# One VectorE for the norm steps, constants in TensorE's waits, and bias rows that are copied per head

## The chip, the cores and the metric

The kernel runs on one core of a Trainium2 chip. The metric is the device time of one execution in microseconds (us); the time before is a median of three runs. TensorE is called PE here, VectorE DVE, ScalarE ACT, GpSimd POOL, and SyncE, whose queue loads the weights, SP.

## The reference, cut to what matters

256 tokens of 1024 values, with 16 meta tokens ahead of them, pass through two layers of a first model and one of a second. A layer of the first model ends each of its halves with a norm that is added to the stream, and the next half begins with another norm of the sum:

```python
def rms_norm(x, g):
    y = xf * lax.rsqrt(jnp.mean(xf * xf, axis=-1, keepdims=True) + EPS)
    return (y * g).astype(x.dtype)

for l in range(DEPTH):                       # 2 layers
    u = rms_norm(h, norm_mix_pre[l])
    proj = u @ w_in[l]                       # retention and attention branches, gates
    ...
    mix = (sigmoid(gate_r) * y_r + sigmoid(gate_a) * y_a) @ w_mix_o[l]
    h = h + rms_norm(mix, norm_mix_post[l])
    u = rms_norm(h, norm_ff_pre[l])
    ff = square(relu(u @ w_ff1[l])) @ w_ff2[l]
    h = h + rms_norm(ff, norm_ff_post[l])
```

The second model projects the 256 tokens to eight stick-breaking and eight dilated heads (the latter with a bias from a table of 32 buckets by distance), multiplies by `w_out`, normalizes, chooses two of 16 experts for each token (`softmax`, best group of four, best two in it), and adds the experts' gated products. All inputs are float32.

## The kernel before, in words

Everything is held with features on the 128 partitions and tokens along the free dimension: `h` has 8 blocks (`KB`) of 128 features by 272 tokens (`L`), or 256 where the meta tokens are no longer needed (`c0`, `s`). The 128x1024 weight blocks (512 KB each) come in order through `Stream` on SP's queue, into four `raw` buffers; `parts` (L72) cuts each in two halves of 512 columns and splits them in a high part `wh` (ACT, L79) and a low part `wl` (L80), three buffers of each. `get` may be told the two engines that make the halves of `wl`: the input projections (`project`, L338, for the blocks 3 to 16), the mixer's `project` (L832) and `w_out` give the second half to POOL, all others have DVE for both.

A dense product takes three passes of a weight block over the tokens, `mm3` (L99): `wh` with the high part of the tokens (L106), `wh` with their low part (L107), `wl` with their high part (L108). 24 of them make an output block of 128 features. Where three output blocks run side by side at the start of a stage (`project`, `ff1`), they take each feature block `kb` in turn, so that PE can begin with the first feature block of a norm.

Four times PE waits for a norm: after the mixing product and after the second feed-forward product of both layers. `sumsq` (L138) sums the squares of the product's blocks, `token_rs` (L153) sums over features with a product of constants (`c_mean`, L159 and L160) and computes 1/sqrt with ACT's logarithm and exponential and one Newton step (`newton`, L166, into `rs_b`). `add_to_h` (L759) then scales the product `f`, adds it to `h` and splits the result into `uh` and `ul` (`xh` and `xl` ahead of the mixer) for the next product. It makes the first block by a way of its own: POOL computes `hg` (L765) and `fy` (L768) beside the Newton step, DVE finishes with L770 and L773. For the other blocks each engine scales (L780) and adds (L781); POOL does the blocks 3 and 6, DVE the rest; ACT makes `uh` (L787) and DVE `ul` (L788). The squares of the new `h` are summed on POOL (L148), for the next norm's factor, which is multiplied in behind the product.

The bias of the dilated heads has one row of 384 values per head (`bias_rows`, L267), formed from the table in the first layer's gates. One DMA on ACT's queue (L279) writes each of the 8 rows 128 times to `scratch` in DRAM, and a later load reads a band with shifted rows from it (`band`, in `mixer_constants`, L221).

The router (L1227 on) forms the choice of experts on DVE out of PE's logits (`po`, L1101), takes counts by products, and gathers each expert's tokens by products (L1274). The weights of the experts, 201 MB, are then loaded in order into buffers that the mixer gave back.

The order on each engine is set by a scheduler that takes the code's order and its dependencies; `add_manual_dep` adds an order without a wait. No table is written out by hand.

Of the kernel before, what the change touches and what calls it, by code (L numbers as in the profile page):

```python
# [19 lines left out]
KB = 8  # L20
META = 16
SEQ = 256
# [23 lines left out]
EXP_LN_SET = 6  # L46
WEIGHTS = ["early"] * 2 + ["early2"] + ["big"] * 8 + ["big2"] * 3 + ["big", "big2"] + ["ring"] * 3 + ["big"] + ["ring2"] * 3
# [39 lines left out]
class Kern:  # L87
    def __init__(self, tc, a, out, dbg=None):
        self.tc, self.nc, self.a, self.out, self.dbg = tc, tc.nc, a, out, dbg or {}
        self.naux = self.ndense = 0  # L90
        self.h_on_pool = None
# [46 lines left out]
    def sumsq(self, acc, src, kb, c0, engine):  # L138
# [9 lines left out]
        x = engine.tensor_tensor(acc[:, c0:], acc[:, c0:], sq[:, c0:], op=ALU.add)  # L148
        if engine is nc.gpsimd and self.h_on_pool is not None:
            self.tc.add_manual_dep(x.ins, self.h_on_pool.ins.name, self.nosync, reason="the sums' own part first")  # L150
        return None

    def token_rs(self, acc, sq, c0):  # L153
# [6 lines left out]
        nc.tensor.matmul(pb[:, :n], self.c_mean, sq[:, c0:], start=False, stop=True)  # L160
# [106 lines left out]
    def bias_rows(self):  # L267
# [9 lines left out]
        nc.vector.tensor_tensor(row[:SB], ps[:SB, :384], lc[:SB], op=ALU.add)  # L277
        self.scratch = self.dram.tile([SB, 128, 384], F32, name="scratch")
        nc.scalar.dma_start(self.scratch, row[:SB].unsqueeze(1).broadcast_to([SB, 128, 384]))  # L279


    def first_layer(self, l):
# [43 lines left out]
        def pre_norm():  # L326
            acc = tp.tile([128, L], F32, name="acc", bufs=1)
            for kb in range(KB):
                sq = self.sumsq(acc, h[:, kb], kb, 0, nc.gpsimd if l else nc.vector)
# [8 lines left out]
        def project(names, s):  # L338
# [5 lines left out]
            both = (nc.vector, nc.gpsimd) if 3 <= done[0] <= 16 else None  # L344
            ws = [st.get(base + C_IN + j, engines=both, after=self.norm_steps if len(c) == 3 == j + 1 else None) for j in c]
            pts = [self.dense_tile() if done[0] < 7 else self.mm_tile() for _ in c]
            for kb in range(KB):
                for (wh, wl), ps in zip(ws, pts):
                    self.mm3(ps[:, :L - s], (hi(wh), hi(wl)), (lambda k: uh[:, k, s:], lambda k: ul[:, k, s:]),
                             [(kb, kb)], kb == 0, kb == KB - 1)  # L350
# [343 lines left out]
        def out_blocks(f, acc, blocks, first_chunk, nk, x, g):  # L694
# [8 lines left out]
            for b, ps in zip(blocks, pts):  # L703
                sq = self.sumsq(acc, ps[:, :n], b, c0, nc.vector)
# [9 lines left out]
        rs1 = self.token_rs(acc, sq, c0)  # L714
# [7 lines left out]
        ux = (lambda k: uh[:, k, c0:], lambda k: ul[:, k, c0:])  # L722

        def ff1(blocks):
            ws = [st.get(base + C_FF1 + b, after=self.norm_steps if b == 2 else None) for b in blocks]
            pts = [self.dense_tile() for _ in blocks]
            for kb in range(8):
                for (wh, wl), ps in zip(ws, pts):
                    self.mm3(ps[:, :n], (hi(wh), hi(wl)), ux, [(kb, kb)], kb == 0, kb == 7)
# [11 lines left out]
        for kb in range(KB):  # L741
            sq = self.sumsq(acc2, h[:, kb, c0:], kb, c0, nc.gpsimd)
# [13 lines left out]
        rs3 = self.token_rs(acc, sq, c0)  # L756
        self.pending = (f, rs3, c0)

    def add_to_h(self, f, rs, c0, uh, ul, g=None, s=0):  # L759

        nc, h = self.nc, self.h
        r, (_, y, t) = rs, rs
        hg = self.tmp("hg", tag="Q", bufs=2)
        g0 = 1.0 if g is None else g[:, :1]
        nc.gpsimd.tensor_scalar(hg, h[:, 0], g0, None, op0=ALU.mult)  # L765

        fy = self.tmp("fy")
        nc.gpsimd.tensor_tensor(fy[:, c0:], f[:, 0, c0:], y[:, c0:], op=ALU.mult)  # L768
        a = self.tmp("t_h")
        nc.vector.scalar_tensor_tensor(a[:, c0:], t[:, c0:], 1.5, fy[:, c0:], op0=ALU.add, op1=ALU.mult)  # L770
        if s < c0:
            nc.scalar.activation(uh[:, 0, :c0 - s], hg[:, s:c0], AF.Copy)
        x = nc.vector.scalar_tensor_tensor(uh[:, 0, c0 - s:], a[:, c0:], g0, hg[:, c0:], op0=ALU.mult, op1=ALU.add)  # L773
        self.norm_steps.append(x)
        rs = self.newton(r, c0)
        for kb in range(KB):
            e = nc.gpsimd if kb in (3, 6) else nc.vector
            if kb:
                a = self.tmp("t_h")
                e.tensor_tensor(a[:, c0:], f[:, kb, c0:], rs[:, c0:], op=ALU.mult)  # L780
            x = e.tensor_tensor(h[:, kb, c0:], h[:, kb, c0:], a[:, c0:], op=ALU.add)  # L781
            if kb == 6:
                self.h_on_pool = x
            x = h[:, kb, s:]
            gk = 1.0 if g is None else g[:, kb:kb + 1]
            if kb:
                nc.scalar.activation(uh[:, kb], x, AF.Copy, scale=gk)  # L787
            nc.vector.scalar_tensor_tensor(ul[:, kb], x, gk, uh[:, kb].bitcast(F32), op0=ALU.mult, op1=ALU.subtract)  # L788
# [35 lines left out]
    def mixer(self):  # L824
# [7 lines left out]
        def project(n):  # L832

            both = (nc.vector, nc.gpsimd)
            ws = [st.get(done[0] + j, engines=both, after=self.norm_steps if n == 3 == j + 1 else None) for j in range(n)]
            done[0] += n
            pts = [self.mm_tile() for _ in ws]
            for kb in range(KB):
                for (wh, wl), ps in zip(ws, pts):
                    self.mm3(ps[:, :SEQ], (hi(wh), hi(wl)), (lambda k: xh[:, k], lambda k: xl[:, k]),  # L840
                             [(kb, kb)], kb == 0, kb == KB - 1)
# [247 lines left out]
        def routed(j):  # L1089

            xt2 = st.raw_pool.tile([128, 1024], F32, name="raw", bufs=st.n_raw)
            for jj in range(2):
# [6 lines left out]
                for i in range(4):  # L1099
                    kb, t = 4 * j + 2 * jj + i // 2, i % 2  # L1100
                    mm(pl[:, NE * t:NE * t + NE], xt[:, 128 * i:128 * i + 128], self.wr[:, kb],  # L1101
                       start=(i == jj == j == 0), stop=(kb == KB - 1), skip_group_check=True)

        for half in range(2):
            for c in range(4):
# [3 lines left out]
                wh, wl = st.parts(w_out[4 * half + c], 256, (nc.vector, nc.gpsimd))  # L1109
                for kb in range(4):  # L1110
                    for t in range(2):
                        ps = po[t][c // 2][:, 256 * (c % 2):256 * (c % 2) + 256]
                        yh, yl = (y[half][:, i, kb, 128 * t:128 * t + 128] for i in range(2))
                        mm(ps, yh, wh[:, kb], start=False, stop=False, skip_group_check=True)
                        mm(ps, yl, wh[:, kb], start=False, stop=False, skip_group_check=True)
                        mm(ps, yh, wl[:, kb], start=False, stop=(half == 1 and kb == 3), skip_group_check=True)
# [64 lines left out]
    def router(self):  # L1181
# [43 lines left out]

        pp = self.bank("pu_")
# [316 lines left out]
    def run(self):  # L1543
        tc, nc = self.tc, self.nc
        pool = lambda name, bufs=1, **kw: tc.tile_pool(name=name, bufs=bufs, reuse_waits="tile", **kw)
        with pool("cp") as self.cp, pool("hp") as self.hp, pool("dram", space=DRAM) as self.dram, \
# [3 lines left out]
            with pool("big", 10) as self.big, ExitStack() as last, ExitStack() as psum:  # L1550
                self.pp = psum.enter_context(pool("pp", space=PSUM))
                with right("raw") as raw, right("part") as part:
# [166 lines left out]
```

## Time and profile before

| | |
|---|---|
| Median of 3 runs | 1568.73 us (1567.92 to 1570.1) |
| Profiled execution: its own time | 1566.69 us |
| Profiled execution: span | 1564.9 us |
| Granted clock of PE, mean | 0.974 |
| PE busy | 1464.6 us, 94% of the span |
| DVE, ACT, POOL busy | 830.8, 731.2, 138.0 us |
| DMA | 363.84 MB, 232 GB/s over the span |

The page says which engine is busy and which stretches lose time. Where a table by stretch is shown, PE's busy time against the length of the stretch is the loss, and the granted clock says whether the products inside run at 2.4 GHz (1.00) or at 1.2 GHz (0.50). A row of a timeline has the start of an instruction, its duration, its engine and its line, and in brackets how long the engine was idle before it and what it waited for. POOL's spans are rough.

### The profile page before, as it was taken

The page shows a single profiled execution, that of the slowest core. Times are in us where ns is not written, and L with a number is a line of the kernel's source. Part 1 is how long each engine was busy: PE and PEld are TensorE (multiplying, and loading weights), DVE is VectorE, ACT ScalarE, POOL GpSimd, SP SyncE. Part 2 cuts the span into 40 slices and gives each one's busy share as a digit, 9 for nine tenths or more (in the row PEclk, how much of TensorE's full clock was granted, in tenths as well). Part 3 has the DMA queues.
Part 4 walks back from the last instruction along what each step waited for, and adds up shares of the span by engine and source line. Part 5 has one row for each costly group of instructions (what it writes and reads, how often), then busy time and mean ns, then how long its engine had stood idle before and what let it go on. Part 6 is the DMA issues. An engine that isn't in the chain of part 4 may idle for free. (4 is left out here: it accounts for less than half of the span.)

```text
span 1564.9 us, 25740 instructions
## 1 busy us (share of the span) xinstructions
PE 1464.6 (94%) x10003; PEld 1150.2 (74%) x10003; DVE 830.8 (53%) x1814; ACT 731.2 (47%) x1646; POOL 138.0 (9%) x132
## 2 busy tenths in 40 slices
PE   7899799899998889999899998999899999999896
PEld 6888699799997788999799997888533334333322
DVE  8877676777445877876787545775301000101002
ACT  7765464566444767674576444875311011101101
POOL 3200000200003320000200003322000000000000
PEclk9999899899998989999899998999999999999999
DMA  6424544365555333445365556547799999999995
GB/s 215 138 97 127 133 138 142 128 195 169 173 174 192 121 122 97 144 152 163 108 202 187 182 186 203 187 162 317 315 419 420 419 420 419 420 419 421 419 419 237
DMA packets 77065, 363.84 MB, mean 232 GB/s; under 512 B 10096, under 2 KB 13192, under 8 KB 52616
## 3 DMA queue, kind: packets, MB, share of 16 engines
q1 hardware_dynamic: 75760, 360.52, 62.5%
q10 hardware_dynamic: 1176, 1.61, 0.9%
q8 instruction: 80, 1.31, 0.3%
q14 instruction: 49, 0.40, 0.1%
HBM read 359.47 MB, written 2.62 MB: 231 GB/s over the span
## 5 line engine op out<-in xcount | busy, mean ns | idle before, releaser
L79 ACT ACTIVATE wh<-raw 128x512 fp32r<-128x512 f32 x576 | 338.6, 625 | 291.6 <-PE mm L107 158.2
L80 DVE TENSOR_TENSOR wl<-raw,wh 128x512 fp32r<-128x512 f32 x519 | 357.2, 710 | 169.4 <-ACT wh L79 160.0
L106 PE MATMUL mm<-uh,wh 128*128 128x272 f32 (+1 forms) x1048 | 312.7, 299 | 21.3 <-DVE uh L773 12.0
L107 PE MATMUL mm<-ul,wh 128*128 128x272 f32 (+1 forms) x1048 | 306.1, 292 | 7.3 <-DVE ul L788 7.3
L108 PE MATMUL mm<-uh,wl 128*128 128x272 f32 (+1 forms) x1048 | 306.4, 292 | 6.1 <-DVE wl L80 4.7
L106 PEld LDWEIGHTS mm<-uh,wh 128*128 128x128 f32 x1048 | 202.9, 194 | 29.5 <-DVE uh L773 13.2
L107 PEld LDWEIGHTS mm<-ul,wh 128*128 128x128 f32 x1048 | 203.0, 194 | 10.0 <-DVE ul L788 8.9
L108 PEld LDWEIGHTS mm<-uh,wl 128*128 128x128 f32 x1048 | 202.7, 193 | 9.2 <-DVE wl L80 7.1
L80 POOL TENSOR_TENSOR wl<-raw,wh 128x512 fp32r<-128x512 f32 x57 | 76.9, 1353 | 453.8 <-ACT wh L79 421.0
L108 PE MATMUL mm<-sh,wl 128*128 128x256 f32 (+1 forms) x352 | 100.3, 285 | 0.0
L107 PE MATMUL mm<-sl,wh 128*128 128x256 f32 (+1 forms) x352 | 100.2, 285 | 0.0
L106 PE MATMUL mm<-sh,wh 128*128 128x256 f32 (+1 forms) x352 | 100.1, 284 | 0.0
L108 PEld LDWEIGHTS mm<-sh,wl 128*128 128x128 f32 x352 | 66.5, 189 | 0.0
L106 PEld LDWEIGHTS mm<-sh,wh 128*128 128x128 f32 x352 | 66.4, 189 | 0.0
L107 PEld LDWEIGHTS mm<-sl,wh 128*128 128x128 f32 x352 | 66.2, 188 | 0.0
L106 PE MATMUL mm<-xh,wh 128*128 128x256 f32 x192 | 55.7, 295 | 6.6 <-DVE xh L773 4.4
L108 PE MATMUL ps<-uh,wl 128*128 128x272 f32 (+1 forms) x200 | 58.4, 292 | 0.3 <-DVE wl L80 0.3
L106 PE MATMUL ps<-uh,wh 128*128 128x272 f32 (+1 forms) x200 | 58.4, 292 | 0.0
L107 PE MATMUL ps<-ul,wh 128*128 128x272 f32 (+1 forms) x200 | 58.2, 291 | 0.0
L107 PE MATMUL mm<-xl,wh 128*128 128x256 f32 x192 | 55.2, 288 | 1.6 <-DVE xl L788 1.6
L108 PE MATMUL mm<-xh,wl 128*128 128x256 f32 x192 | 54.9, 287 | 0.2 <-DVE wl L80 0.2
L108 PE MATMUL ps<-sh,wl 128*128 128x272 f32 (+1 forms) x160 | 45.8, 286 | 0.0
(686 smaller groups left out, 3009.1 us busy)
## 6 DMA issues: line engine op xcount, KB each, us to landing
raw<-in_w_first SPq DMA_DIRECT2D x288, 512.0 KB, 3.5
we_big<-in_w_exp SPq DMA_DIRECT2D x115, 1024.0 KB, 19.9
we_ring<-in_w_exp SPq DMA_DIRECT2D x48, 1024.0 KB, 19.9
we_early<-in_w_exp SPq DMA_DIRECT2D x27, 1024.0 KB, 19.9
wo<-in_w_first SPq DMA_DIRECT2D x4, 512.0 KB, 5.6
we_big<-in_w_exp SPq DMA_DIRECT2D x4, 512.0 KB, 18.1
scratch<-row ACTq DMA_DIRECT2D x1, 1536.0 KB
h<-in_hT SPq DMA_DIRECT2D x4, 272.0 KB, 5.2
```

What stands on the lines that cost most here:

```text
L79: x = nc.scalar.activation(wh[:, c], raw[:, c], AF.Copy)
L80: y = engines[j // 512].tensor_tensor(wl[:, c], raw[:, c], wh[:, c].bitcast(F32), op=ALU.subtract)
L106: mm(ps, wh(kw), xh(kx), start=f, stop=False)
L107: mm(ps, wh(kw), xl(kx), start=False, stop=False)
L108: mm(ps, wl(kw), xh(kx), start=False, stop=l)
```

## The change

Four things change.

*The norm steps.* `add_to_h` works in three steps: `part` (L795 of the new kernel) scales a block of the product, `add` (L800) adds it to `h`, `low` (L803) makes `ul` of the block before. All are on DVE; `hg` moves to ACT. The own way of the first block is left out: its Newton step is done first, then `part` and `uh` (L808). The sums of squares and all halves of `wl` are on DVE too. POOL keeps the retention's distance (L445) and the memsets.

*The order of the products.* `mm3s` replaces `mm3` in the input projections, the first feed-forward product and the mixer's projection. Over the output blocks of a group it issues all `wh` with high parts, then all `wl` with high parts, then all `wh` with low parts. The last chunk of `w_out` goes by token tile instead of by feature block.

*Constants.* `keep_on` issues 13 products of the 128x128 constant `c_mean` with itself, into a PSUM bank that nobody reads. It stands at the start, behind the sum product of the four norms (`token_rs` with `keep`) and in the router behind the logits.

*The bias rows.* The 8 rows go to DRAM once (`bias_row`, ACT's queue). In the first feed-forward product of layer 0, behind the blocks 20 to 27, SP's queue copies one row 128 times to `scratch`, DRAM to DRAM.

```diff
+KEEP = 13
+    def mm3s(self, pts, n, ws, xs, kb, first, last):
+        xh, xl = xs
+        mm = self.nc.tensor.matmul
+        for ps, (wh, wl) in zip(pts, ws):
+            mm(ps[:, :n], wh[:, kb], xh, start=first, stop=False)
+        for ps, (wh, wl) in zip(pts, ws):
+            mm(ps[:, :n], wl[:, kb], xh, start=False, stop=False)
+        for ps, (wh, wl) in zip(pts, ws):
+            mm(ps[:, :n], wh[:, kb], xl, start=False, stop=last)
...
+    def keep_on(self, n, tag, after, psum=None):
+        ps = (psum or self.psum)(tag)
+        for _ in range(n):
+            x = self.nc.tensor.matmul(ps[:, :128], self.c_mean, self.c_mean, start=True, stop=True)
+            if after is not None:
+                self.tc.add_manual_dep(x.ins, after.ins.name, self.nosync, reason="in the wait")
+            after = x
...
-        nc.tensor.matmul(pb[:, :n], self.c_mean, sq[:, c0:], start=False, stop=True)
+        x = nc.tensor.matmul(pb[:, :n], self.c_mean, sq[:, c0:], start=False, stop=True)
+        if keep:
+            self.keep_on(keep, "pz", x)
...
-        nc.scalar.dma_start(self.scratch, row[:SB].unsqueeze(1).broadcast_to([SB, 128, 384]))
+        nc.scalar.dma_start(self.bias_row, row[:SB])
+    def bias_copies(self, hd):
+        self.load(self.scratch[hd:hd + 1], self.bias_row[hd:hd + 1].unsqueeze(1).broadcast_to([1, 128, 384]))
...
-            both = (nc.vector, nc.gpsimd) if 3 <= done[0] <= 16 else None
...
+            if l == 0 and 20 <= b < 28:
+                self.bias_copies(b - 20)
...
-        nc.gpsimd.tensor_scalar(hg, h[:, 0], g0, None, op0=ALU.mult)
-        nc.gpsimd.tensor_tensor(fy[:, c0:], f[:, 0, c0:], y[:, c0:], op=ALU.mult)
-        nc.vector.scalar_tensor_tensor(a[:, c0:], t[:, c0:], 1.5, fy[:, c0:], op0=ALU.add, op1=ALU.mult)
+        nc.scalar.activation(hg, h[:, 0], AF.Copy, scale=gk(0))
+        rs = self.newton(rs, c0)
...
-            e = nc.gpsimd if kb in (3, 6) else nc.vector
...
+        for kb in range(1, KB):
+            part(kb)
+            add(kb)
+            nc.scalar.activation(uh[:, kb], h[:, kb, s:], AF.Copy, scale=gk(kb))
+            low(kb - 1)
+        low(KB - 1)
...
+        self.keep_on(13, "pg_", self.routed, self.bank)
```

**PE, where the mixing product of layer 0 ends and the first feed-forward product begins.** `po` is the bank of the norm's sum, `mm` and `ps` are the banks of the output blocks, `pz` the one of the constants. Before:

```order
L159 MATMUL po<-acc,c_mean 128x272
L160 MATMUL po<-sq,c_mean 128x272
L106 MATMUL mm<-uh,wh 128x272 x2
L106 MATMUL ps<-uh,wh 128x272
L107 MATMUL mm<-ul,wh 128x272
L108 MATMUL mm<-uh,wl 128x272
```

After:

```order
L178 MATMUL po<-acc,c_mean 128x272
L179 MATMUL po<-sq,c_mean 128x272
L167 MATMUL pz<-c_mean 128x128 x13
L116 MATMUL mm<-uh,wh 128x272 x2
L116 MATMUL ps<-uh,wh 128x272
L118 MATMUL mm<-uh,wl 128x272 x2
L120 MATMUL mm<-ul,wh 128x272 x2
```

Behind the sum's product the 13 constants now stand ahead of the first product of the tokens, and the third output block (`ps`) has only its first pass there; its others follow when the first two blocks are done.

**DVE, the same norm.** `rs_*` are the steps of 1/sqrt, `t_h` is the scaled product. Before:

```order
L187 TENSOR_SCALAR rs_h_3516<-po_3510,eps_73 128x272
L189 TENSOR_TENSOR rs_t_3515<-rs_y_3514 128x272
L190 TENSOR_TENSOR rs_t_3515<-rs_t_3515,rs_h_3516 128x272
L770 SCALAR_TENSOR_TENSOR t_h_3528<-rs_t_3515,fy_3526 128x272
L169 SCALAR_TENSOR_TENSOR rs_b_3513<-rs_t_3515,rs_y_3514 128x272
L773 SCALAR_TENSOR_TENSOR uh_3522<-t_h_3528,gvec_66,hg_3524 128x272
L781 TENSOR_TENSOR h_68<-h_68,t_h_3528 128x272
L780 TENSOR_TENSOR t_h_3534<-f_3215,rs_b_3513 128x272
L788 SCALAR_TENSOR_TENSOR ul_3523<-h_68,gvec_66,uh_3522 128x272
L781 TENSOR_TENSOR h_68<-h_68,t_h_3534 128x272
L780 TENSOR_TENSOR t_h_3539<-f_3215,rs_b_3513 128x272
L780 TENSOR_TENSOR t_h_3549<-f_3215,rs_b_3513 128x272
```

After:

```order
L208 TENSOR_SCALAR rs_h_3545<-po_3525,eps_73 128x272
L210 TENSOR_TENSOR rs_t_3544<-rs_y_3543 128x272
L211 TENSOR_TENSOR rs_t_3544<-rs_t_3544,rs_h_3545 128x272
L190 SCALAR_TENSOR_TENSOR rs_b_3542<-rs_t_3544,rs_y_3543 128x272
L795 TENSOR_TENSOR t_h_3556<-f_3230,rs_b_3542 128x272
L808 SCALAR_TENSOR_TENSOR uh_3551<-t_h_3556,gvec_66,hg_3553 128x272
L800 TENSOR_TENSOR h_68<-h_68,t_h_3556 128x272
L795 TENSOR_TENSOR t_h_3560<-f_3230,rs_b_3542 128x272
L803 SCALAR_TENSOR_TENSOR ul_3552<-h_68,gvec_66,uh_3551 128x272
L800 TENSOR_TENSOR h_68<-h_68,t_h_3560 128x272
L795 TENSOR_TENSOR t_h_3565<-f_3230,rs_b_3542 128x272
L795 TENSOR_TENSOR t_h_3570<-f_3230,rs_b_3542 128x272
```

The step that waited for POOL's `fy` (L770) is gone; the first block's scaling stands in its place behind the Newton step, and the blocks follow one another with no place for POOL's.

**SP, the first feed-forward product of layer 0.** `raw` are weight blocks. Before:

```order
L221 DMA lnr_4299<-in_ln_rows 16x256
L64 DMA raw_4303<-in_w_first 128x1024
L64 DMA raw_4342<-in_w_first 128x1024
L64 DMA raw_4381<-in_w_first 128x1024
L64 DMA raw_4420<-in_w_first 128x1024
L64 DMA raw_4459<-in_w_first 128x1024
L64 DMA raw_4498<-in_w_first 128x1024
```

After:

```order
L242 DMA lnr_4326<-in_ln_rows 16x256
L66 DMA raw_4330<-in_w_first 128x1024
L66 DMA raw_4369<-in_w_first 128x1024
L66 DMA raw_4408<-in_w_first 128x1024
L66 DMA raw_4447<-in_w_first 128x1024
L242 DMA scratch_1861<-bias_row_1860 128x1x384
L66 DMA raw_4487<-in_w_first 128x1024
```

A copy of a bias row now stands between two weight blocks, and seven more follow in the same way, one behind each block.

## Rows read from the trace of the kernel before

**Rows 1.** The page, busy us of each engine (share of the span) and instructions:

```profile
PE 1464.6 (94%) x10003; PEld 1150.2 (74%) x10003; DVE 830.8 (53%) x1814; ACT 731.2 (47%) x1646; POOL 138.0 (9%) x132
```

**Rows 2.** Stretches: us; busy PE, PEld, DVE, ACT, POOL; PEclk, DMA share, GB/s.

```profile
154.00:162.00 8.00, 7.86 (x70) 7.25 (x71) 4.83 (x16) 5.11 (x16) 0.00 (x0) 1.00 0.46 59
162.00:180.00 18.00, 8.11 (x66) 7.88 (x64) 6.32 (x20) 4.46 (x13) 0.00 (x0) 0.83 0.66 130
...
340.00:400.00 60.00, 60.00 (x479) 60.00 (x478) 44.74 (x85) 38.17 (x81) 3.10 (x2) 1.00 0.53 171
...
620.00:640.00 20.00, 20.00 (x157) 17.58 (x156) 19.42 (x64) 13.41 (x40) 0.00 (x0) 1.00 0.33 104
```

**Rows 3.** Stretches: each norm, its last L160 product's end to the 97th product.

```profile
286.90:311.26 24.36, 17.70 (x102) 15.98 (x101) 20.89 (x35) 12.09 (x27) 9.65 (x11) 0.79 0.18 59
494.69:520.98 26.29, 17.78 (x102) 15.83 (x101) 20.09 (x31) 13.73 (x31) 13.16 (x14) 0.81 0.13 38
761.93:785.13 23.20, 16.84 (x100) 15.34 (x101) 19.82 (x34) 11.82 (x27) 9.08 (x11) 0.78 0.18 58
956.87:980.25 23.38, 14.93 (x96) 13.89 (x96) 18.09 (x34) 10.15 (x25) 10.10 (x9) 0.78 0.65 216
```

**Rows 4.** Stretches: input projections of layers 0 and 1, and the mixer.

```profile
20.00:80.00 60.00, 51.01 (x367) 48.27 (x366) 53.02 (x95) 44.59 (x99) 20.27 (x16) 0.94 0.41 136
...
520.00:580.00 60.00, 50.32 (x359) 47.52 (x358) 52.70 (x95) 43.64 (x98) 17.98 (x14) 0.91 0.41 132
...
980.00:1100.00 120.00, 116.52 (x916) 105.10 (x917) 80.59 (x207) 86.94 (x215) 34.36 (x28) 1.00 0.63 229
```

**Rows 5.** Stretches: the router, and the expert phase.

```profile
1109.00:1116.00 7.00, 3.41 (x20) 3.35 (x20) 4.20 (x25) 3.05 (x5) 0.00 (x0) 0.51 1.00 421
...
1120.00:1546.00 426.00, 413.01 (x1932) 155.46 (x1930) 41.23 (x88) 51.16 (x96) 0.00 (x0) 1.00 1.01 416
```

**Rows 6.** Timeline of the gates: start, us, engine, line, operation, count [idle <-releaser].

```profile
147.52 1.28 ACTq L279 DMA_DIRECT2D scratch<-row  x1
...
179.49 0.63 ACT L79 ACTIVATE wh<-raw 128x512 fp32r<-128x512 f32 x1 [13.19 <-DMA raw<-in_w_first]
...
180.45 0.90 PE L536 MATMUL pz<-ident,s_a 128*128 128x128 f32 x3 [10.34 <-ACT pt_a L537]
```

**Rows 7.** The page, DMA queue: packets, MB, share of 16 engines.

```profile
q10 hardware_dynamic: 1176, 1.61, 0.9%
```

**Rows 8.** Timeline of the first norm.

```profile
290.64 0.82 PE L106 MATMUL mm<-uh,wh 128*128 128x272 f32 x2 [3.74 <-DVE uh L773]
...
291.29 0.84 POOL L781 TENSOR_TENSOR h<-h,t_h 128x272 f32<-128x272 f32 x1
...
291.43 1.00 DVE L780 TENSOR_TENSOR t_h<-f,rs_b 128x272 f32<-128x272 f32 x1
...
293.40 0.59 PE L107 MATMUL mm<-ul,wh 128*128 128x272 f32 x1 [1.71 <-DVE ul L788]
```

**Rows 9.** Timeline of the second norm, two additions while POOL rests.

```profile
502.87 0.78 DVE L780 TENSOR_TENSOR t_h<-f,rs_b 128x272 f32<-128x272 f32 x2
```

**Rows 10.** Timeline of the router.

```profile
1111.82 0.17 PE L1227 MATMUL pu__13604<-r_mb,utri 128*128 128x16 bf16 x1 [3.34 <-DVE r_mb L1216]
...
1112.87 2.47 PE L1274 MATMUL misc<-sel,x 128*128 128x128 f32 x10 [0.77 <-ACT x L1223]
...
1116.13 1.95 PE L1274 MATMUL pd__13631<-sel,x 128*128 128x128 f32 x16
```

**Rows 11.** Stretches: inside the first norm, right behind its low clock.

```profile
301.00:304.00 3.00, 2.00 (x14) 1.62 (x13) 3.00 (x4) 1.28 (x3) 2.47 (x3) 1.00 0.00 0
```

**Rows 12.** Groups by line: count | busy us, mean ns | idle, releaser.

```profile
L80 POOL TENSOR_TENSOR wl<-raw,wh 128x512 fp32r<-128x512 f32 x11 | 15.0, 1361 | 27.6 <-ACT wh L79 18.2 <-issue 5.9 <-PE mm L108 3.4
L80 POOL TENSOR_TENSOR wl<-raw,wh 128x512 fp32r<-128x512 f32 x12 | 16.8, 1412 | 30.9 <-ACT wh L79 13.1 <-DVE ks_r L368 5.4 <-DVE roped L361 4.7
L80 DVE TENSOR_TENSOR wl<-raw,wh 128x512 fp32r<-128x512 f32 x74 | 49.3, 685 | 11.3 <-ACT wh L79 10.7
```

More of the change, by code (lines that the diff above doesn't have):

```diff
@@ L136, in aux_tile, with sumsq @@
         return self.psum("ps" if self.naux % 2 else "pz")
-    def sumsq(self, acc, src, kb, c0, engine):
+    def sumsq(self, acc, src, kb, c0):
         nc = self.nc
@@ L147, in sumsq, with token_rs @@
             return sq
-        x = engine.tensor_tensor(acc[:, c0:], acc[:, c0:], sq[:, c0:], op=ALU.add)
-        if engine is nc.gpsimd and self.h_on_pool is not None:
-            self.tc.add_manual_dep(x.ins, self.h_on_pool.ins.name, self.nosync, reason="the sums' own part first")
-        return None
-    def token_rs(self, acc, sq, c0):
+        nc.vector.tensor_tensor(acc[:, c0:], acc[:, c0:], sq[:, c0:], op=ALU.add)
+        return None
+    def keep_on(self, n, tag, after, psum=None):
[5 more added lines that the diff above has]
+            after = x
+    def token_rs(self, acc, sq, c0, keep=0):
         nc = self.nc
@@ L343, in project @@
             c = range(done[0] - len(names), done[0])
[L344 to L345 removed]
+            ws = [st.get(base + C_IN + j, after=self.norm_steps if len(c) == 3 == j + 1 else None) for j in c]
             pts = [self.dense_tile() if done[0] < 7 else self.mm_tile() for _ in c]
             for kb in range(KB):
[L348 to L350 removed]
+                self.mm3s(pts, L - s, ws, (uh[:, kb, s:], ul[:, kb, s:]), kb, kb == 0, kb == KB - 1)
             return pts
@@ new lines, in add_to_h, with part, add @@
+        if s < c0:
+            nc.scalar.activation(uh[:, 0, :c0 - s], h[:, 0, s:c0], AF.Copy, scale=gk(0))
+        rs = self.newton(rs, c0)
+        parts = {}
+        def part(kb):
+            a = parts[kb] = self.tmp("t_h")
+            z = nc.vector.tensor_tensor(a[:, c0:], f[:, kb, c0:], rs[:, c0:], op=ALU.mult)
+            if kb:
+                self.tc.add_manual_dep(z.ins, x.ins.name, self.nosync, reason="the first block first")
+        def add(kb):
+            nc.vector.tensor_tensor(h[:, kb, c0:], h[:, kb, c0:], parts[kb][:, c0:], op=ALU.add)
@@ new lines, in low @@
+        def low(kb):
+            nc.vector.scalar_tensor_tensor(ul[:, kb], h[:, kb, s:], gk(kb), uh[:, kb].bitcast(F32), op0=ALU.mult,
+                                           op1=ALU.subtract)
+        part(0)
+        x = nc.vector.scalar_tensor_tensor(uh[:, 0, c0 - s:], parts[0][:, c0:], gk(0), hg[:, c0:], op0=ALU.mult,
+                                           op1=ALU.add)
+        self.norm_steps.append(x)
+        add(0)
+        for kb in range(1, KB):
[3 more added lines that the diff above has]
+            low(kb - 1)
@@ L832, in project @@
         def project(n):
-            both = (nc.vector, nc.gpsimd)
-            ws = [st.get(done[0] + j, engines=both, after=self.norm_steps if n == 3 == j + 1 else None) for j in range(n)]
+            ws = [st.get(done[0] + j, after=self.norm_steps if n == 3 == j + 1 else None) for j in range(n)]
             done[0] += n
@@ L1108, in mixer @@
                         head_scale(k)
[L1109 to L1116, printed above, removed]
+                wh, wl = st.parts(w_out[4 * half + c], 256)
+                ends = half == 1 and c == 3
+                for i in range(8):
+                    kb, t = (i % 4, i // 4) if ends else (i // 2, i % 2)
+                    ps = po[t][c // 2][:, 256 * (c % 2):256 * (c % 2) + 256]
+                    yh, yl = (y[half][:, x, kb, 128 * t:128 * t + 128] for x in range(2))
+                    mm(ps, yh, wh[:, kb], start=False, stop=False, skip_group_check=True)
+                    mm(ps, yl, wh[:, kb], start=False, stop=False, skip_group_check=True)
+                    mm(ps, yh, wl[:, kb], start=False, stop=(half == 1 and kb == 3), skip_group_check=True)
                 if half == 1 and c == 1:
```

45 lines of the change are left out of this document (12 added, 33 removed).

## The prediction

> **What bounds the kernel now.** I read first the busy times of the whole span: PE is busy 1464.6 of 1564.9 us, the other engines about half or less [rows 1]. So a gain can only come from the 100 us in which PE is idle, or from products that run at half clock. Next come stretches: the table by stretch gives for each PE's busy time, the granted clock and the DMA share. A healthy stretch of dense products (340 to 400) reads PE 60.00 of 60 at clock 1.00 [rows 2]. Four kinds of stretch don't: one in the first layer's gates (162 to 180: PE 8.11 of 18, [rows 2]), the four norms that stand between dense stages [rows 3], the input projections of both layers [rows 4], and the router [rows 5]. The change touches all four. After the router the expert phase is bound by DMA (share 1.01 at 416 GB/s over 426 us, [rows 5]): its length doesn't change, but it starts when the mixer's buffers come free, so time won earlier is passed on to the end.
>
> **Part 1, the bias rows.** Before, one DMA on ACT's queue writes 1024 pieces of 1536 bytes from eight partitions at 147.52. From 154 to 162 the DMA engines are 0.46 busy and move only 59 GB/s. ACT then waits 13.19 us for a weight block (until 179.49) and PE 10.34 us (until 180.45) [rows 2, 6]. At the same place in layer 1, where nothing of the kind runs, PE is 20.00 of 20 busy (620 to 640, [rows 2]). The queue's packets took 0.9% of 16 engines' span, 225 us of packet time, or 0.22 us each for the thousand pieces [rows 7]. After: eight rows to DRAM (8 pieces) at this place, so the stall goes. Worth: 10.34 us of waiting, and about 14 products that then run at half clock; a product takes 0.126 us at full clock in the trace's dense stretches (60 us for 479 records [rows 2]) and about twice that at half, so 14 x 0.126 = 1.8. Together 12; lower end 8, if the DMA backlog of the next block is what PE meets instead.
>
> The same 1024 pieces come back as eight copies of 128, ahead of one weight block each, in the first feed-forward product of layer 0, on SP's queue, the one that brings the weights. There PE is at 60.00 of 60 and DMA at 0.53 [rows 2]: of a block's 3.0 us (24 products of 0.126), 1.4 us of DMA time are free. A copy of 128 pieces over 16 engines costs 8 x 0.22 = 1.76 us. The surplus is 0.35 us a block, 2.8 us in all; four raw buffers give 12 us of lead. So I take **0**, and bound it by 0 and 14 us (8 x 1.76, nothing hidden).
>
> A wide spread is what this rests on. Before, the engines' share of 0.46 says that seven or eight of 16 worked, as many as the transfer has source rows [rows 2]. The Trainium skill (DMA: Bandwidth & Descriptors, "Why a DMA increments its semaphore by 16 and not by 1") has the number of engines as the largest divisor up to 16 of the slowest dimension on both sides that isn't of size one. By that rule 8 before, with which the trace agrees, and 16 for the copies, whose leading dimension is one and whose second is 128; no run here shows the copies. The same page ("Queues, rings and completion order") has each engine take a queue's pieces in the order of issue, so a copy on SP's queue holds back the weights behind it in full; that speaks against this part, and by it a copy that isn't hidden costs its whole 1.76 us.
>
> **Part 2, the four norms.** From the end of the last product of the sum of squares to the 97th product behind it, the four take 24.36, 26.29, 23.20 and 23.38 us, of which PE is busy 17.70, 17.78, 16.84 and 14.93 at a mean clock of 0.78 to 0.81 [rows 3]. 96 products at full clock are 12.1 us; the rest is loss. In the first norm PE waits 3.74 us for the first block and 1.71 for its low part [rows 8]. While POOL works on its two blocks, DVE's instructions take 1.00 us (POOL's 0.84 each beside them) [rows 8]; two of the same kind without POOL take 0.78 together [rows 9]. So 0.84 us of POOL costs DVE about 0.57, and PE's feed is DVE.
>
> After: everything is on DVE. Per block a part, an addition and a low part: 0.35 + 0.37 + 0.41 = 1.13 us apart, an estimate from the 0.39 each of [rows 9] and of PE's order. The chain to the first block keeps its length: two instructions of POOL go, one on DVE comes, and the factor (hg) moves to ACT, in a gap that it has before its logarithm. So the first product comes about 3.4 us after the sum instead of 3.74. The other seven blocks at 1.13 are there 11.3 us after the sum, and with the two halves of the third output block's low weights (0.685 each [rows 12]) it is 12.6. In that time PE has the products of two output blocks, 6 x 0.126 = 0.76 us in each 1.13. Some 27 products, nearly all of the third output block, follow at 0.126: 16.0 us. Behind the 72nd product come 24 more, 3.0 us, and 0.8 for the sums of the next norm (an estimate), 3.8 to the 97th: **20.0** us in norms 1 and 2. Norm 3 has 256 columns and gives 19, norm 4 has no sums behind it and gives 18. Gains 4.4, 6.3, 4.2, 5.4: **20 us**. This holds if the clock stays up. 13 products of constants (26 instructions, the 16 of [rows 10] take 1.95 us, so 0.12 each) fill 3.1 us of the 3.4 us wait; they end before the first block is there and push nothing back. At two thirds busy the clock stayed at 1.00 in a stretch right behind [rows 11]. If it falls, the 72 products cost 0.10 us more each where they bound: 27 x 0.10 + the feed 8 x 0.23 = 4.5 us, at most half of it unhidden, so a norm gives about 2.5 less: range 10 to 24.
>
> **Part 3, all low weights on DVE.** In the input projections DVE is 53.02 and 52.70 of 60 busy, and PE 51.01 and 50.32 [rows 4]. POOL makes 11 and 12 low halves there, 15.0 and 16.8 us [rows 12]. They move to DVE at 0.685 us [rows 12]: +7.5 and +8.2. What goes is POOL's share of the slowing, 0.57/0.84 x 15.0 = 10.2 and x 16.8 = 11.4. Net 2.7 and 3.2 us less, **6 us**. Ends: +14 (slowing isn't won back where DVE reads PSUM) and -4 again. In the mixer the halves move to a DVE that is 80.59 of 120 busy [rows 4], beside a PE at 116.52: 0, bound by 2 each way.
>
> **Part 4, the router and the start.** PE waits 3.34 us for the choice of experts [rows 10]; from 1109 to 1116 the clock is 0.51 [rows 5]. Of the gather that follows, 16 products take 1.95 us at full clock against 2.47 us for the 10 ahead of them [rows 10]. 26 constants fill the wait, and the last output product comes in another order: 1 us gained, from -2 (the constants run at half clock themselves, 26 x 0.25 = 6.4, and hold up the counts) to +2. At the start 13 constants stand ahead of the first weights: 0, -1 to +1.
>
> **The sum.** 12 + 20 + 6 + 1 = 39 off the profiled execution's 1566.69 (span 1564.9 and 1.8 around it): 1527.7. The median of the runs is 1568.73, 2.0 above it, so **1530 us**.
>
> **Rivals.** *The clock falls all the same* behind the constants: norms give 20 - 10 = 10, 1540. For: the low stretches begin where PE waits. Against: [rows 11]. *DVE becomes the bound*: it takes 23 halves in the projections, 15.7 us, and wins nothing back, so +15.7 in place of -6: 1552. For: DVE at 53 of 60. Against: the 1.00 us instructions. *The stall only moves*: the copies hold the weights up by the bound of 14 us, 1544. For: one queue, DMA already at 0.53. *Slower than before*: each copy stays on a single engine, since its source is one row, and every weight block is spread over 16 and waits for the last one. Then a copy lasts 128 x 0.22 = 28 us, eight 225 us, against 24 us of products: 1530 + 200 = 1730. It decides from about 8 us a copy (39 gained + 24 hidden over eight), that is with three engines or fewer. For: before, the engines were as many as the source's rows [rows 2]. Against: a source of one row is spread over its 128 repeats in the access pattern of the built program; before, the first counted dimension was the 8. *It goes better*: the projections keep the clock as well and win 12 us more, 1518.
>
> **How the numbers follow.** Forecast 0.52 (1530, itself 1522 to 1537), clock 0.19 (1540), DVE 0.09 (1552), moved stall 0.08 (1544), single engine 0.06 (1730), better 0.06 (1518). I leave out the single engine and most of what lies above 1550: range 1514 to 1552. A measurement here tells 0.2%, 3.1 us, from no change. Faster 0.92, same 0.02 (DVE's rival with part 1 lost), slower 0.06.
>
> **What would show it.** Right: around 165 to 180 PE has no wait above 2 us; the bias copies land within 4 us and PE stays near 20 of 20 in the stretch that holds them; DVE has no 1.00 us instruction in a norm; sum to 97th product 18 to 20 us at a clock near 1.00; the input projections shorter by some 3 us a layer; POOL's low halves gone. Wrong: low weights that end PE's waits in the projections, a clock of 0.5 behind a norm, waits on raw in the feed-forward blocks 20 to 28.

## The result, and the profile after

The changed kernel takes 1552.25 us (median of four runs, 1551.72 to 1555.22) against 1568.33 for the kernel before beside it: a ratio of 0.990 with a 95% interval of 0.9883 to 0.9917. It is 16 us faster. I had forecast 1530 in a range of 1514 to 1552: the gain is 16 of the 39 us forecast, and the time lies just outside the range. The profiled execution has a span of 1549.6 us against 1564.9.

The page of the changed kernel: busy time of each engine, and its DMA issues (count, KB each, median us from issue to landing).

```profile
PE 1478.6 (95%) x10159; PEld 1161.7 (75%) x10159; DVE 831.2 (54%) x1909; ACT 727.4 (47%) x1650; POOL 19.2 (1%) x29
...
raw<-in_w_first SPq DMA_DIRECT2D x288, 512.0 KB, 3.5
...
scratch<-bias_row SPq DMA_DIRECT2D x8, 192.0 KB, 4.3
```

PE has 156 products more than before [rows 1], the constants, and is busy for 14 us more, in part because of them; POOL fell from 138.0 to 19.2. Each copy lands 4.3 us after its issue, a weight block 3.5.

The table by stretch of the changed kernel answers to [rows 2 to 4]: the gates, the input projections of both layers, the four norms from the sum's last product to the 97th behind it, and four stretches of the first feed-forward product of layer 0. Columns: length, busy us (count) of PE, PEld, DVE, ACT, POOL, granted clock, DMA share, GB/s.

```profile
162.00:180.00 18.00, 18.00 (x156) 17.51 (x155) 15.24 (x47) 12.35 (x37) 0.00 (x0) 1.00 0.44 145
...
20.00:80.00 60.00, 55.66 (x416) 52.53 (x415) 53.33 (x115) 48.23 (x105) 5.90 (x6) 1.00 0.48 156
520.00:580.00 60.00, 54.67 (x409) 52.20 (x409) 53.40 (x117) 47.90 (x107) 2.48 (x3) 0.97 0.43 141
...
266.28:286.74 20.46, 18.02 (x128) 16.01 (x127) 18.85 (x44) 12.59 (x28) 0.00 (x0) 1.00 0.18 66
501.23:523.43 22.20, 18.47 (x126) 16.02 (x126) 18.84 (x45) 14.36 (x32) 0.00 (x0) 1.00 0.14 42
756.99:776.67 19.68, 17.35 (x128) 15.43 (x127) 18.07 (x45) 12.35 (x28) 0.00 (x0) 1.00 0.20 67
948.40:969.01 20.61, 16.56 (x123) 14.53 (x121) 16.75 (x42) 10.38 (x25) 0.00 (x0) 1.00 0.69 249
...
320.00:330.00 10.00, 10.00 (x82) 10.00 (x81) 8.04 (x17) 5.63 (x13) 1.36 (x1) 1.00 0.76 218
340.00:360.00 20.00, 14.47 (x70) 13.30 (x71) 6.09 (x11) 5.04 (x11) 0.00 (x0) 0.74 0.33 107
360.00:380.00 20.00, 13.15 (x71) 11.79 (x70) 6.54 (x12) 5.70 (x12) 0.00 (x0) 0.83 0.26 81
380.00:400.00 20.00, 15.38 (x104) 14.52 (x103) 11.12 (x20) 9.47 (x20) 0.00 (x0) 0.91 0.40 131
```

Three of the four parts show in their places. The gates are full (18.00 of 18, 8.11 before [rows 2]). The norms take 20.46, 22.20, 19.68 and 20.61 us (24.36, 26.29, 23.20 and 23.38 before [rows 3]) at a clock of 1.00. PE has 55.66 and 54.67 us of 60 in the projections (51.01 and 50.32 [rows 4]; the second stretch lies 6.5 us earlier in the program here, since the second norm comes later). But the first feed-forward product of layer 0, which was 60.00 of 60 before (340 to 400 [rows 2]), now has 14.47, 13.15 and 15.38 of 20, at a DMA share of 0.26 to 0.40. Between the ends of the first and of the second norm's sum lie 234.95 us (266.28 to 501.23) against 207.79 before (286.90 to 494.69). With the 3.9 us that the first norm gained, 31 us were lost here. From 340 to 400 PE did 245 products where it did 479 before; at the old pace these are 31 us of work. Of the 29 us lost in this stretch 17 are idle (43.00 busy of 60), and some 12 went into the products themselves, at the lower clock.

The hole has an odd look. DMA is emptier than before, and no row there waits for a transfer. The timeline of SP and ACT, with one row of PE, shows what happens (start, us, engine, line, operation, in brackets the idle time before it and what ended it; rows in order of time, others left out):

```profile
322.45 0.33 SPq L66 DMA_DIRECT2D raw<-in_w_first  x1
...
329.76 1.16 ACT L81 ACTIVATE wh<-raw 128x512 fp32r<-128x512 f32 x2 [1.68 <-PE ps L120]
...
333.74 0.43 ACT L757 ACTIVATE s_ff<-r_ff 128x272 f32<-128x272 f32 x1 [1.11 <-DVE r_ff L755]
...
336.29 0.43 ACT L757 ACTIVATE s_ff<-r_ff 128x272 f32<-128x272 f32 x1 [1.66 <-DVE r_ff L755]
...
339.32 0.43 ACT L757 ACTIVATE s_ff<-r_ff 128x272 f32<-128x272 f32 x1 [2.13 <-DVE r_ff L755]
...
340.11 1.14 ACT L81 ACTIVATE wh<-raw 128x512 fp32r<-128x512 f32 x2
346.69 0.43 ACT L757 ACTIVATE s_ff<-r_ff 128x272 f32<-128x272 f32 x1 [5.44 <-DVE r_ff L755]
...
347.49 1.13 ACT L81 ACTIVATE wh<-raw 128x512 fp32r<-128x512 f32 x2
...
348.15 0.39 PE L116 MATMUL mm<-uh,wh 128*128 128x272 f32 x1 [1.97 <-ACT wh L81]
```

The block that is split at 340.11 was asked for at 322.45; a weight block lands after 3.5 us (the median), so it had been there for some 14 us. ACT didn't wait for it: no wait stands in that row. ACT took it late, because three outputs of earlier blocks (L757 at 333.74, 336.29, 339.32) stand ahead of it in ACT's fixed order, with no weights between them. These used up the lead, the weights that had been split before PE needed them. From there on the order is weights, then the output of that same block, then the next weights, so one block passes through ACT, DVE and PE in turn: 7.4 us from one split to the next (340.11 to 347.49) instead of 3.0. PE waits 1.97 or 1.98 us for `wh` in each turn, and the granted clock of the stretches is 0.74 to 0.91.

### The profile page after: what moved, and what is told of

Its sections match the earlier page's. It is cut to its first block, busy times and chain, and to the rows that moved or that the text cites. A ratio compares the mean times of both kernels' runs of the same rounds, so it can differ in the third digit from the quotient of the medians.

```text
span 1549.6 us, 25893 instructions
## 1 busy us (share of the span) xinstructions
PE 1478.6 (95%) x10159; PEld 1161.7 (75%) x10159; DVE 831.2 (54%) x1909; ACT 727.4 (47%) x1650; POOL 19.2 (1%) x29
## 5 line engine op out<-in xcount | busy, mean ns | idle before, releaser
L81 ACT ACTIVATE wh<-raw 128x512 fp32r<-128x512 f32 x576 | 342.4, 624 | 272.6 <-PE mm L108 84.7
L82 DVE TENSOR_TENSOR wl<-raw,wh 128x512 fp32r<-128x512 f32 x576 | 384.9, 687 | 149.8 <-ACT wh L81 139.4
L116 PE MATMUL mm<-uh,wh 128*128 128x272 f32 (+1 forms) x1048 | 309.6, 297 | 19.6 <-ACT wh L81 14.4
L118 PE MATMUL mm<-uh,wl 128*128 128x272 f32 (+1 forms) x1048 | 302.6, 290 | 5.5 <-DVE wl L82 5.5
L120 PE MATMUL mm<-ul,wh 128*128 128x272 f32 (+1 forms) x1048 | 302.7, 290 | 1.5 <-DVE ul L803 0.6
L757 ACT ACTIVATE s_ff<-r_ff 128x272 f32<-128x272 f32 (+1 forms) x64 | 26.4, 413 | 41.3 <-DVE r_ff L755 41.3
```

The source lines that it names most:

```text
L81: x = nc.scalar.activation(wh[:, c], raw[:, c], AF.Copy)
L82: y = engines[j // 512].tensor_tensor(wl[:, c], raw[:, c], wh[:, c].bitcast(F32), op=ALU.subtract)
L116: mm(ps[:, :n], wh[:, kb], xh, start=first, stop=False)
L118: mm(ps[:, :n], wl[:, kb], xh, start=False, stop=False)
L120: mm(ps[:, :n], wh[:, kb], xl, start=False, stop=last)
L757: nc.scalar.activation(s[:, c0:], r[:, c0:], AF.Square)
```

## The experiments

Line numbers shift by a few from kernel to kernel.

**Theory (order):** the copies changed the scheduler's order on ACT and DVE, and this order costs the 31 us; the copies as transfers cost nothing. **Rival (transfer):** the copies hold back the weights on SP's queue.

**The copies elsewhere.** Only their place is another:

```diff
-            if l == 0 and 20 <= b < 28:
-                self.bias_copies(b - 20)
...
             sq = out_blocks(f, acc, [b], base + C_FF2, 32, sx, g_ff_post)
+            if l == 0:
+                self.bias_copies(b)
```

> The changed kernel with its eight bias copies behind the blocks of the second feed-forward product of layer 0 instead of behind blocks 20 to 27 of the first. Theory (order): in the changed kernel the 31 us between the first and the second norm are lost because ACT's fixed order puts the high weights of the next block behind the previous block's output; here ACT's order in the first product is again weights, output, weights, output, and in the second product no output stands between. Expect about 1521 us, and PE 20 of 20 in both products. Rival (transfer): the copies hold back the weight loads on their queue wherever they stand, so the loss moves with them: about 1552 us, with a hole of about 30 us in the second product.

Measured: 1550.27 us, so by the numbers the rival's. The profile says otherwise for the largest hole. Rows of SP, PE and ACT, and a stretch of the second norm:

```profile
473.84 4.70 SPq L66 DMA_DIRECT2D raw<-in_w_first  x4
...
501.48 1.27 PE L178 MATMUL po<-acc,c_mean 128*128 128x272 f32 x2 [11.97 <-DVE acc L160]
...
504.55 1.66 ACT L81 ACTIVATE wh<-raw 128x512 fp32r<-128x512 f32 x3
```

```profile
490.00:500.00 10.00, 0.00 (x0) 0.00 (x0) 9.86 (x28) 5.57 (x13) 0.00 (x0) 0.59 0.00 1
```

PE is idle for the whole stretch. Behind the constants the next instruction in its order is now the following norm's sum (L178), which needs all eight blocks of this norm; in the changed kernel 72 products of the tokens stand ahead of it. ACT's order has changed too: the weights asked for at 473.84 and after are split only at 504.55, behind all eight blocks. The first product was full again (20.00 of 20 from 320 to 380). PE also has holes in the second product (16.81 to 18.84 of each 20 us from 380 to 480), and what makes these isn't shown. Since the copies changed the order here as well, this run doesn't tell the theories apart.

**The copies where they are, ACT's order mended.** The weights of the next block are split ahead of a block's output, by an order without a wait; first with one block of lead, later with two (the cut is that of two):

```diff
+            self.part_last = x
...
-            nc.scalar.activation(s[:, c0:], r[:, c0:], AF.Square)
+            x = nc.scalar.activation(s[:, c0:], r[:, c0:], AF.Square)
+            if ahead:
+                tc.add_manual_dep(x.ins, ahead.pop().ins.name, self.nosync, reason="the next weights first")
...
             (ps,) = ff1([b])
+            if l == 0 and 17 <= b < 30:
+                for j in (base + C_FF1 + b + 1, base + C_FF1 + b + 2):
+                    if j not in st.ready:
+                        st.ready[j] = st.get(j)
+                ahead.append(st.part_last)
             ff1_out(b, ps, rs2)
```

> The changed kernel with its bias copies left where they are; only the weights of the next block are split ahead of the output of the block before (a forced order on ACT, blocks 18 to 30 of layer 0). Theory (order): one block of lead is back, so PE waits little in blocks 20 to 30: 1521 to 1526 us. Rival (transfer): the copies still stand in the queue, so 1552 us as in the changed kernel.

> As the first kernel with a forced order (the eight copies stay behind blocks 20 to 27 of the first feed-forward product), but with two blocks of weights split ahead of a block's output instead of one. The first one still had eight waits of 1.0 us on the low weights there. Theory (order): with full lead nothing of the copies is left: 1520 to 1522 us, PE 20 of 20 from 320 to 400. Rival (transfer has a part): the copies' own 14 us or less stay, 1526 to 1531 us.

Measured: 1530.56 us with one block of lead, above the 1521 to 1526 expected of the theory, and 1519.04 with two. With one block PE still waits for the low weights, eight times 1.0 us. Its waits from 330 to 400 (total, times, longest):

```profile
PE mm L119 <- DVE wl L82: 5.0, 5, 1.0
PE ps L119 <- DVE wl L82: 3.0, 3, 1.0
```

And the product with two blocks:

```profile
340.00:360.00 20.00, 20.00 (x161) 20.00 (x160) 12.05 (x24) 12.80 (x27) 0.00 (x0) 1.00 0.60 191
360.00:380.00 20.00, 20.00 (x161) 20.00 (x160) 14.22 (x27) 11.65 (x24) 0.00 (x0) 1.00 0.66 203
380.00:400.00 20.00, 20.00 (x161) 20.00 (x161) 8.41 (x15) 8.96 (x18) 0.00 (x0) 1.00 0.56 169
```

The eight copies move the same bytes at the same place of the program, and PE is full. The transfers cost nothing that can be measured.

**The old transfer, and the bad order without copies.** The first kernel takes back part 1 alone; the second adds to it the kind of order that the changed kernel has, and no copy (the cut is what it adds; `out_last` is the split output of the block before):

```diff
+            late = self.out_last if l == 0 and 21 <= blocks[0] <= 30 else None
-            ws = [st.get(base + C_FF1 + b, after=self.norm_steps if b == 2 else None) for b in blocks]
+            ws = [st.get(base + C_FF1 + b, after=self.norm_steps if b == 2 else late) for b in blocks]
...
-            self.split(sh[b // 8][:, b % 8, c0:], sl[b // 8][:, b % 8, c0:], s[:, c0:])
+            self.out_last = self.split(sh[b // 8][:, b % 8, c0:], sl[b // 8][:, b % 8, c0:], s[:, c0:])
```

> The changed kernel with the bias transfer of before (one transfer of 1024 pieces from eight partitions on ACT's queue, in the gates). Both theories: no hole in the first feed-forward product, the 10 us wait and the low clock of before are back in the gates (12 us): 1552 - 31 + 12 = 1533 us. It prices the first part of the change and shows what the other parts are worth together: 1568 - 1533 = 35 us.

> As the kernel with the old bias transfer, without any copies in the first feed-forward product, but with ACT's and DVE's order forced there to what the changed kernel has: the weights of blocks 21 to 30 behind the output of the block before. Theory (order): about 7 us a block for ten blocks in place of 3, so 30 us more than the kernel with the old transfer, about 1564 us. Rival (transfer): no copies, no loss: 1533 us.

Measured: 1534.01 and 1572.75 us. The order alone costs 38.7 us, more than the 30 expected, and makes a kernel with all gains but that of the bias rows slower than the one before (ratio 1.0031, interval 1.002 to 1.0043). It holds for ten blocks (splits from 343.22 to 415.64), the changed kernel's for eight (329.76 to 388.00): that is about 4 us a block in both. Its table by stretch and ACT's timeline look like those of the changed kernel:

```profile
360.00:380.00 20.00, 13.58 (x72) 12.19 (x72) 6.28 (x12) 5.68 (x12) 0.00 (x0) 0.83 0.24 79
380.00:400.00 20.00, 13.38 (x72) 12.17 (x72) 6.34 (x12) 5.70 (x12) 0.00 (x0) 0.83 0.25 79
```

```profile
367.03 0.43 ACT L758 ACTIVATE s_ff<-r_ff 128x272 f32<-128x272 f32 x1 [5.12 <-DVE r_ff L756]
367.49 0.43 ACT L97 ACTIVATE sh<-s_ff 128x272 fp32r<-128x272 f32 x1
367.82 1.13 ACT L81 ACTIVATE wh<-raw 128x512 fp32r<-128x512 f32 x2
```

The order is shown from both sides: with copies and good order no loss, with bad order and no copies the loss. Why the scheduler gives the copies such an order isn't shown by any run; that it plans with durations of its own for them is a guess.

**One copy for all heads** in place of the eight, behind the fourth block of the second feed-forward product:

```diff
+        x = self.nc.sync.dma_start(self.scratch.rearrange("h p c -> p h c"), self.bias_row.unsqueeze(0).broadcast_to([128, SB, 384]))
+        self.tc.add_manual_dep(x.ins, self.stream.last.ins.name, self.nosync, reason="the weights first")
...
+            if l == 0 and b == 3:
+                self.bias_all()
```

> The changed kernel with the eight copies made one: a single transfer of 128 x 8 rows from DRAM to DRAM, behind the fourth block of the second feed-forward product of layer 0. ACT's order in both feed-forward products is that of the kernel with the old bias transfer. Theory (order): nothing of the 31 us is left and the gates have no wait either: 1534 - 12 = 1521 us. Rival (transfer): 1024 pieces in one go hold the weights back for longer than eight times 128: a hole of 5 to 14 us in the second product, 1526 to 1535 us.

Measured: 1520.22 us. The copy of 1536 KB lands in 10.1 us beside the weights, while PE is full:

```profile
scratch<-bias_row SPq DMA_DIRECT2D x1, 1536.0 KB, 10.1
```

```profile
425.00:435.00 10.00, 10.00 (x81) 10.00 (x80) 4.65 (x8) 4.12 (x8) 0.00 (x0) 1.00 0.51 182
435.00:445.00 10.00, 10.00 (x82) 10.00 (x81) 3.88 (x6) 3.91 (x7) 0.00 (x0) 1.00 0.52 164
```

With it as the base, each of the other parts was taken back alone.

**Part 1 alone, on the kernel before:** its bias rows, with the single copy.

> The kernel before with the bias rows of the change alone, brought back by the single copy in the second feed-forward product. My prediction: 12 us less than before, 1556 us; the gates at 160 to 180 without a wait above 2 us, nothing new elsewhere.

Measured: 1554.30 us, 13.5 less than before. The gates:

```profile
162.00:180.00 18.00, 18.00 (x157) 17.49 (x155) 14.40 (x45) 11.80 (x33) 0.00 (x0) 1.00 0.43 147
```

**The constants** left out (`KEEP` 0, and the calls at the start and in the router):

> The same with the single copy, without the products of constants (start, four norms, router). If the constants hold the clock, each norm loses what half clock costs behind it: 2.5 us by my prediction, 10 in all, and 1 or 2 in the router: about 1533 us. If the clock stays up without them, because PE is fed faster now: 1521 us.

Measured: 1522.62 us, 2.4 more (1521.69 to 1523.43 against 1519.43 to 1521.53). The four norms of this kernel, as in [rows 3], a stretch at the end of the second, and PE's largest wait in the router:

```profile
266.63:287.08 20.45, 15.97 (x102) 14.49 (x101) 18.83 (x44) 12.59 (x28) 0.00 (x0) 0.92 0.18 67
470.50:494.21 23.71, 18.36 (x102) 16.89 (x102) 20.34 (x49) 14.36 (x32) 0.00 (x0) 0.78 0.16 54
727.59:747.24 19.65, 15.25 (x101) 13.85 (x102) 18.04 (x45) 12.34 (x28) 0.00 (x0) 0.91 0.19 59
918.97:939.46 20.49, 14.37 (x97) 13.04 (x97) 16.75 (x42) 10.39 (x25) 0.00 (x0) 0.92 0.70 248
...
490.00:492.00 2.00, 2.00 (x10) 2.00 (x10) 2.00 (x6) 2.00 (x5) 0.00 (x0) 0.50 0.22 25
```

```profile
PE pu__13598 L1258 <- DVE r_mb L1247: 3.3, 1, 3.3
```

The clock falls to a mean of 0.78 to 0.92, and three of four norms still take what they take with the constants (20.45, 19.65, 20.49). There the pace is DVE's: in the third norm PE lags behind while its clock is low (0.50 from 733 to 735), catches up at full clock, and waits 0.38 us for the last block, as in the changed kernel (0.37). The second norm loses 1.5 us, where the clock is at 0.50 once more (490 to 492) and the products of the next output block set the pace. The router's 3.3 us wait is back and costs nothing: from the last norm's sum to the end both kernels take 602.6 us (1518.7 - 916.05 and 1521.6 - 918.97).

**The low weights** shared with POOL again (input projections, mixer, `w_out`):

```diff
+            both = (nc.vector, nc.gpsimd) if 3 <= done[0] <= 16 else None
-            ws = [st.get(base + C_IN + j, after=self.norm_steps if len(c) == 3 == j + 1 else None) for j in c]
+            ws = [st.get(base + C_IN + j, engines=both, after=self.norm_steps if len(c) == 3 == j + 1 else None) for j in c]
...
-                wh, wl = st.parts(w_out[4 * half + c], 256)
+                wh, wl = st.parts(w_out[4 * half + c], 256, (nc.vector, nc.gpsimd))
```

> The same with the single copy; the second half of the low weights is on POOL again in the input projections 3 to 16, the mixer's projections and the output projection, as before. My prediction has these 6 us dearer: 1527 us. If POOL's share was a relief for DVE: 1515 us or less.

Measured: 1538.98 us, 18.8 more, and not the 6 expected. Two stages, from the start to the first norm's sum and from the second norm's sum to the third's, with POOL, and then the same stages of the base:

```profile
0.00:274.77 274.77, 260.76 (x1971) 245.44 (x1972) 209.38 (x496) 179.32 (x426) 27.46 (x32) 0.99 0.43 147
478.64:740.92 262.28, 247.80 (x1920) 232.09 (x1919) 207.45 (x484) 172.24 (x414) 23.59 (x19) 0.98 0.39 133
```

```profile
0.00:266.17 266.17, 258.89 (x1971) 244.07 (x1972) 207.17 (x509) 179.32 (x426) 10.20 (x19) 1.00 0.45 151
470.06:724.64 254.58, 244.62 (x1920) 228.84 (x1919) 203.81 (x498) 172.13 (x414) 4.52 (x5) 1.00 0.41 136
```

POOL's share costs 8.6 us in the first stage and 7.7 in the second; 3.3 more lie behind the last norm's sum, in the mixer and `w_out` (606.0 us to the end against 602.65). Without POOL, DVE does 13 and 14 instructions more and is still busy for 2.2 and 3.6 us less. The stages gain more than that: PE's idle time falls by 6.7 and 4.5 us, and the same products take 1.9 and 3.2 us less, at a clock of 1.00 instead of 0.99 and 0.98. How much longer a half takes on DVE beside POOL, the groups of L82 from 20 to 80 show, of that kernel, and then of the changed kernel (mean ns behind the busy time):

```profile
L82 POOL TENSOR_TENSOR wl<-raw,wh 128x512 fp32r<-128x512 f32 x11 | 14.8, 1341 | 27.9 <-ACT wh L81 22.0 <-issue 5.9
L82 DVE TENSOR_TENSOR wl<-raw,wh 128x512 fp32r<-128x512 f32 x18 | 14.2, 800 | 0.0
```

```profile
L82 DVE TENSOR_TENSOR wl<-raw,wh 128x512 fp32r<-128x512 f32 x31 | 20.6, 682 | 0.1
```

**The norm steps** of before (`add_to_h` with POOL, sums on POOL), constants and order of products kept:

> The same with the single copy; the steps of the norm are those of before (POOL makes the first block's factors, two blocks and the sums of squares), with the constants and the new order of products kept. If the work on POOL slows DVE as the rows of before show, each norm loses 2 to 4 us: 1529 to 1537 us. If the constants alone made the gain: 1521 us.

Measured: 1535.37 us, 15.2 more. Its four norms, as in [rows 3]:

```profile
266.51:291.18 24.67, 19.96 (x126) 18.13 (x126) 20.71 (x34) 12.10 (x27) 9.67 (x11) 0.86 0.16 55
474.62:500.90 26.28, 20.29 (x126) 18.18 (x126) 20.70 (x35) 13.75 (x31) 9.66 (x11) 0.87 0.11 36
733.31:756.91 23.60, 18.42 (x127) 16.54 (x126) 19.74 (x35) 11.81 (x27) 9.10 (x11) 0.93 0.16 56
928.65:951.16 22.51, 16.87 (x123) 15.66 (x122) 17.78 (x38) 10.17 (x25) 4.12 (x5) 0.92 0.64 225
```

24.67, 26.28, 23.60 and 22.51 us: 14.2 more than in the base (20.44, 22.19, 19.68, 20.60), and within 1 us of the kernel before, which has no constants. With the constants in all four the clock is still only 0.86 to 0.93 here.

**The order of products** of before in `mm3s`:

> The changed kernel with the single copy, with the order of products of before in the groups (both products of the high weights first, the low weights last, block by block). My prediction gave this order no price of its own: 1520 us. If taking the low weights before the tokens' low parts is what lets PE work on while DVE splits the tokens, each of the four norms loses up to the 1.7 us that PE waited for the first low part before, 7 us: 1527 us.

Measured: 1516.86 us, 3.4 less (1516.05 to 1517.37 against 1519.43 to 1521.53; the intervals of the two ratios to the kernel before just meet). The new order doesn't help, it costs. This kernel is the fastest of all: 0.9671 of the kernel before (0.9654 to 0.9687), 35 us less than the changed one.

## Why the prediction was wrong

It failed in one step, the second half of part 1: "So I take **0**, and bound it by 0 and 14 us". The price of the transfer was right (1519.04 with the copies in place and a good order). What the step left out is that the same eight copies in the code also move instructions on ACT and DVE. I read the order of PE and DVE at the norm and SP's at the copies, and not ACT's at the copies, where three outputs without weights between them stand in plain sight. Measured: 32.0 us (1552.25 - 1520.22), beyond the bound. The prediction's own sign of trouble there, waits on `raw`, didn't appear: PE waited for splits, with the transfers long landed. The rival *The stall only moves* had the right place and the wrong cause and price, 14 us by queued transfers.

Without this the changed kernel would take 1520, 10 us under the forecast, by errors that partly cancel. The other steps, with the measured term behind the forecast one:

- **Bias stall, 12:** 13.5 by the run, 12.3 by the trace (the first norm's sum ends at 274.62 instead of 286.90). Right, and by its mechanism.
- **Norms, 20:** 14.3 by the traces (24.36 - 20.46 and so on: 3.9, 4.1, 3.5, 2.8), 15.2 by the run. The way to the 72nd product was right (16.1 us after the sum in norms 1 and 2, 16.0 forecast). The step that was too short is "3.8 to the 97th": 4.4 us in the first norm, 6.1 in the second, where PE then waits 1.3 us for the next block's weights, and 5.8 in the fourth, where it waits 0.8 us for weights and 1.6 us for DVE (`ks`, L875).
- **Constants:** part 2 had the clock as its condition, 2.5 us a norm. They bring 2.4 in all. In three norms, where DVE sets the pace, the low clock is hidden; in the second it costs 1.5.
- **Low weights, 6:** 18.8. DVE is slower beside POOL, as forecast, and its busy time fell by about what was forecast (2.2 and 3.6 us; 2.7 and 3.2 forecast). The step that was mis-sized takes that for the gain of the stages ("Net 2.7 and 3.2 us less, **6 us**"). They gained 8.6 and 7.7, since PE's idle time and its low clock went too, and the mixer with `w_out`, put at 0 with a bound of 2, gave 3.3. Which waits make up PE's idle time isn't shown; from 20 to 80 it waits for a half of POOL's only once, 1.0 us.
- **Router, 1:** 0 from the constants. The new order of `w_out` alone wasn't tried.
- **Order of products, no price:** it costs 3.4 us. Which stage pays wasn't isolated: the traces differ by 0.1 to 1.5 us in each.

The rivals: the clock rival can't cost 10 us, since without any constants the kernel takes 2.4 more. DVE as the bound had the wrong sign: it took the halves and was busy for less. *It goes better* had the projections nearly right, 10 us more than forecast, of which 5.1 is shorter products; the changed kernel hides it behind the 32 us. A single engine for each copy fell: the copies land in 4.3 us, not 28. The rule of the Trainium skill (DMA: Bandwidth & Descriptors, "Why a DMA increments its semaphore by 16 and not by 1") has 16 engines here. The landing agrees with it as against one engine, but doesn't count the engines.

## What to carry to other kernels

A transfer that is written between the steps of a pipelined loop can cost far more by the order that a scheduler then gives to the engines than by its bytes: compare the order of every engine of that loop, and count how many weights stand ahead of each output. If a stage has holes while DMA is idle and its buffers are full, look at what stands ahead in the waiting engine's queue, not at the transfer. Where one engine is slower beside another, price its share by the length of the whole stage, not by the busy time that it saves: here 2.2 and 3.6 us of DVE's time were worth 8.6 and 7.7 us.

## What the runs showed of the hardware

- DVE is slower beside POOL: a half of the low weights took 800 ns on DVE with POOL at work on the others, 682 ns without. In the same stage DVE did 509 instructions in 207.17 us beside 10.20 us of POOL's work, and 496 in 209.38 us beside 27.46 us.
- A low clock can be free where PE is fed slowly: three norms took the same time at a mean clock of 0.91 to 0.92 as at 1.00. In the second, where products at 0.50 also came behind DVE's last block, 1.5 us were lost.
- Out of eight partitions, 1024 pieces of 1536 bytes held a weight block back until 32 us after their issue (147.52 to 179.49 [rows 6]); with part 1 alone, where they are gone from there, PE is full (18.00 of 18). From DRAM to DRAM, as one copy at another place, 1024 such pieces landed in 10.1 us.
